# The output projection of the prompt as seven block products, with operand sums in DRAM

## The chip, the cores and the metric

The kernel runs on one core of a Trainium2 chip. The metric is the device time of one execution in microseconds (us). Single runs of the kernel before took 2335.16 to 2336.0 us, with a median of 2335.55 us over 3 runs.

## What is computed

One layer of a streaming encoder: RMS norm of x, one input projection into eight parts, stick-breaking attention (8 heads) beside retention (8 heads), a gated per-head norm of both, one output projection, and a norm with a residual. The part that the change touches is the end:

```python
def merge(o_sb, o_r, gate_sb, gate_r, g_sb, g_r, w_out):
    y_sb = head_rms_norm(o_sb, g_sb, gate_sb.dtype) * jax.nn.silu(gate_sb)
    y_r = head_rms_norm(o_r, g_r, gate_r.dtype) * jax.nn.silu(gate_r)
    y = jnp.concatenate([y_sb, y_r], axis=-1)
    return jnp.einsum('bte,ed->btd', y, w_out)
...
        xp = xp + rms_norm(out, norm_post[l])
```

It is done for 1024 prompt frames (8 tiles of 128 rows) and for 8 x 16 sample frames (one tile, "the sample"). y has 2048 columns: 16 blocks of 128, blocks 0 to 7 from the attention heads and 8 to 15 from the retention heads. w_out is 2048 x 2048.

## The kernel before

Every large product is made three times, since an f32 operand is split into a high part (rounded to the format fp32r) and the low rest: hi x hi, hi x lo, lo x hi. `split` (L139 to L141) does it for a weight block: ACT writes the high part (tile `wh`), DVE subtracts it (tile `wl`). The blocks come by SP's queue into `wr`. All three tags live in the pool `wp` with four buffers each (L118), so that the weights run at most four blocks ahead of TensorE at each of the two stages: landed, and converted.

The rows are done in two groups: group 1 has prompt tiles 0 to 3 and the sample, group 2 tiles 4 to 7. In a group each of the eight heads goes through its projections in an order written out by hand (`order`, L207): rq, rk, rv, rg, ret, q, k, v, sg, x. A projection (`products`, L297) uses one weight block of 256 KB for twelve products of 512 columns. The work of the branches, retention and attention, is cut into steps of generators (`Job`, L167) that `tick` (L172) takes up after so many products of TensorE: a `yield 28` means "go on after 28 ticks". `place` (L163) ties an instruction behind the last product in its engine's order. DRAM scratch tiles take the finished y: `s_y[group][block]`, and `s_ys` for the attention blocks of the sample. A scheduler decides the final order on each engine.

The output stage (from L1185 on) works on three chunks of three row tiles: (0, 1, 2), (4, 5, 6) and (3, sample, 7). `fetch` brings a chunk's y from DRAM and converts it, `out_panel` (L1205) makes one panel of 512 columns: for each of 16 blocks of w_out, three tiles x three products (L1222, L1223, L1224). A panel's results are squared by ACT (L1275) and multiplied with the gain by DVE (L1278), `close` scales the finished chunk and adds x (L1304) in steps placed between products of the next chunk. Of the last chunk the last 256 columns are done tile by tile (L1349 to L1351), with weights that `keep_last` has converted before, so that each tile's norm, scaling and stores can follow it.

In terms of block products: rows in two halves (tiles 0 to 3, tiles 4 to 7), y's columns in two halves, w_out's columns in halves too, so the prompt takes eight products of half matrices.

## Time and profile before

| what | value |
|---|---|
| median of 3 runs | 2335.55 us |
| lowest and highest | 2335.16 and 2336.0 us |
| span of the profiled execution | 2332.0 us |
| instructions in it | 39220 |
| first and last start of L1222 | 1922.8 and 2305.7 us |
| DMA, mean | 179 GB/s, 418.55 MB |

The profiled execution has no time of its own on the page, only its span, from its first to its last instruction; the median of the runs lies 3.55 us above it, which is what lies around the span. Engines are PE (TensorE's products), PEld (its weight loads, which run beside the products), DVE (VectorE), ACT (ScalarE), POOL (GpSimd) and SP (the DMA queue); "L302" is line 302 of the kernel. A group's row gives line, engine, operation, tile written and tiles read, shape, count, then busy us and mean ns of one, then the idle time before it and what ended it.

### The profile page before, as it was taken

Reading aid. Unit: us, or ns where it says so; the run is one execution under the profiler, and the core shown is the slowest. Engines: PE = TensorE matmul, PEld = TensorE weight load, DVE = VectorE, ACT = ScalarE, POOL = GpSimd, SP = SyncE. Lnnn points to the kernel's source line nnn. Section 1 sums busy time; section 2 is a strip of 40 time slices with the busy share of each in tenths; the row PEclk is TensorE's granted clock in tenths of the full one; section 3 lists DMA queues with packets and bytes.
Section 4 is the critical chain, followed back from the end, with each engine's and each line's share of the span. In section 5 each row is a group of like instructions: output and inputs, shape, how many; then the busy total and the mean of one; then the engine's idle time right before and its main releaser. Section 6 shows DMA issues by size and latency. Waiting matters only on the chain.

```text
span 2332.0 us, 39220 instructions
## 1 busy us (share of the span) xinstructions
PE 2304.9 (99%) x14256; PEld 2054.3 (88%) x14256; DVE 1336.2 (57%) x2642; ACT 892.7 (38%) x1880; POOL 513.4 (22%) x747
## 2 busy tenths in 40 slices
PE   7999999999999999999999999999999999999998
PEld 7999999999999999998888888888888888888888
DVE  8246564556555564556756655665665566555544
ACT  6323332333333242333443433434343344534342
POOL 2123241414223141423321311122032130010000
PEclk9999999999999999999999999999999999999999
DMA  7659686787869677798966656565565576757564
GB/s 251 166 132 232 165 187 171 187 199 169 204 154 206 175 180 186 172 225 215 225 174 159 154 152 154 136 158 150 150 159 149 138 186 199 239 177 225 173 213 134
DMA packets 696161, 418.55 MB, mean 179 GB/s; under 512 B 234880, under 2 KB 646784, under 8 KB 693536
## 3 DMA queue, kind: packets, MB, share of 16 engines
q1 hardware_dynamic: 632240, 316.27, 51.9%
q0 software_dynamic: 28528, 79.33, 13.9%
q10 hardware_dynamic: 35200, 20.45, 3.1%
q8 instruction: 111, 1.82, 0.3%
q14 instruction: 82, 0.67, 0.1%
HBM read 336.24 MB, written 79.69 MB: 178 GB/s over the span
## 4 chain that ended last, share of the span: by engine, by line
PE 94%; DVE 2%; issue 2%; ACT 1%; DMA 0%; POOL 0%; DVEq 0%; ACTq 0%; POOLq 0%
PE acc L302 51%; PE accn L361 12%; PE a L1222 5%; PE a L1223 5%; PE a L1224 5%; PE accx L389 4%; PE pa L693 3%; PE z L660 2%; PE pd L829 1%; PE zc L764 1%; PE rs L851 1%; DVE kp L603 1%; PE pS L884 1%; PE pa L869 1%; PE pa L874 1%
## 5 line engine op out<-in xcount | busy, mean ns | idle before, releaser
L141 DVE TENSOR_TENSOR wl<-wr,wh 128x512 fp32r<-128x512 f32 (+1 forms) x576 | 392.4, 684 | 561.8 <-ACT wh L140 545.8
L302 PE MATMUL acc<-mh,wl 128*128 128x256 f32 (+2 forms) x2304 | 662.5, 340 | 0.0
L302 PE MATMUL acc<-ml,wh 128*128 128x256 f32 (+2 forms) x2304 | 660.0, 339 | 0.8 <-DVE p0u L153 0.8
L302 PE MATMUL acc<-mh,wh 128*128 128x256 f32 (+2 forms) x2304 | 660.7, 339 | 0.0
L140 ACT ACTIVATE wh<-wr 128x512 fp32r<-128x512 f32 (+1 forms) x576 | 360.3, 626 | 771.8 <-PE acc L302 399.6
L302 PEld LDWEIGHTS acc<-ml,wh 128*128 128x128 f32 x2304 | 421.2, 188 | 36.3 <-issue 6.6
L302 PEld LDWEIGHTS acc<-mh,wl 128*128 128x128 f32 x2304 | 421.1, 188 | 36.4 <-issue 8.2
L302 PEld LDWEIGHTS acc<-mh,wh 128*128 128x128 f32 x2304 | 421.7, 188 | 34.5 <-issue 6.6
L745 POOL DMA_DIRECT2D kc<-cache_sb_k x256 | 166.5, 655 | 283.1 <-DVE kcT L776 131.7
L361 PE MATMUL accn<-whn,mh 128*128 128x256 f32 x768 | 223.9, 292 | 0.0
L1222 PE MATMUL a<-wh,mh 128*128 128x512 f32 (+1 forms) x576 | 219.7, 381 | 0.1
L1223 PE MATMUL a<-wl,mh 128*128 128x512 f32 (+1 forms) x576 | 219.2, 380 | 0.0
L1224 PE MATMUL a<-wh,ml 128*128 128x512 f32 (+1 forms) x576 | 219.1, 380 | 0.0
L361 PE MATMUL accn<-wln,mh 128*128 128x256 f32 x768 | 217.0, 283 | 0.0
L361 PE MATMUL accn<-whn,ml 128*128 128x256 f32 x768 | 216.9, 283 | 0.0
L361 PEld LDWEIGHTS accn<-whn,mh 128*128 128x128 f32 x768 | 146.6, 191 | 9.8 <-issue 7.9
L361 PEld LDWEIGHTS accn<-wln,mh 128*128 128x128 f32 x768 | 146.6, 191 | 0.3
L603 DVE TENSOR_TENSOR_SCAN kp<-kp 128x640 f32<-128x640 f32 (+6 forms) x72 | 108.4, 1505 | 66.5 <-POOL kp L592 63.9
L361 PEld LDWEIGHTS accn<-whn,ml 128*128 128x128 f32 x768 | 146.4, 191 | 0.0
L1222 PEld LDWEIGHTS a<-wh,mh 128*128 128x128 f32 x576 | 108.3, 188 | 20.8 <-DVE sg L406 0.3
L1224 PEld LDWEIGHTS a<-wh,ml 128*128 128x128 f32 x576 | 108.3, 188 | 20.5
L1223 PEld LDWEIGHTS a<-wl,mh 128*128 128x128 f32 x576 | 108.3, 188 | 20.3
(209 smaller groups left out, 2968.5 us busy)
## 6 DMA issues: line engine op xcount, KB each, us to landing
wr<-w_in SPq DMA_DIRECT2D x384, 256.0 KB, 3.9
wr<-w_out SPq DMA_DIRECT2D x184, 256.0 KB, 3.6
vc<-cache_sb_v SPq DMA_DIRECT2D x64, 512.0 KB, 7.5
wrn<-w_in SPq DMA_DIRECT2D x80, 256.0 KB, 3.7
kc<-cache_sb_k SPq DMA_DIRECT2D x256, 64.0 KB, 3.9
kc<-cache_sb_k POOLq DMA_DIRECT2D x256, 64.0 KB, 4.2
wrx<-w_in SPq DMA_DIRECT2D x48, 256.0 KB, 3.0
xt<-x_prompt SPq DMA_DIRECT2D x8, 1024.0 KB, 5.4
```

The source lines that it names most:

```text
L140: nc.scalar.activation(hi, src, AF.Copy)
L141: nc.vector.tensor_tensor(lo, src, hi.bitcast(F32), ALU.subtract)
L302: last = nc.tensor.matmul(a[:, :m], lhs[:, j, :], rhs[w][:, j, o : o + m], start=(w == 0 and j == 0 and n == 0), stop=(w == KT // WQ - 1 a ...
L361: product[0] = nc.tensor.matmul(a, lhs[q][:, jj, ts], rhs[:, j, :], start=(w == 0 and j == 0 and n == 0 and t % 2 == 0), stop=(w == KT // ...
L389: product[0] = nc.tensor.matmul(banks[t], lhs[q][:, j, ts], rhs, start=(k == 0 and n == 0), stop=(k == KT - 1 and n == 2))
L603: nc.vector.tensor_tensor_scan(rev, rev, rev, 1.0, ALU.mult, ALU.bypass)
L660: mm = nc.tensor.matmul(z[:, :c], q2[a][:, i * P : (i + 1) * P], k2[b][:, :c], start=(m == 0), stop=(m == 2))
L693: nc.tensor.matmul(po[:, :P], at[:, j, :], rest["vn"][:, j, :], start=(j == 0), stop=(j == t))
L745: (nc.gpsimd if i < 2 else nc.sync).dma_start(kc[32 * i : 32 * i + 32, :].rearrange("p (k d) -> p k d", d=32), cache_k[0, 2 * c + j, s * 5 ...
L1222: nc.tensor.matmul(a[:, :width], hi[q][:, j, ts], wh, start=(k == 0), stop=False)
L1223: nc.tensor.matmul(a[:, :width], hi[q][:, j, ts], wl, start=False, stop=False)
L1224: product[0] = nc.tensor.matmul(a[:, :width], lo[q][:, j, ts], wh, start=False, stop=(k == KT - 1))
```

## The change

The prompt's output projection is done with seven instead of eight half-matrix products, in Winograd's form of Strassen's scheme. The products are named 1 to 7. Product 1 takes y's block a11 (tiles 0 to 3, attention columns) and the w_out block of the same rows, 2 takes a12, 4 takes a22; 3, 5, 6 and 7 take sums of blocks of y (s4, S1, S2, s3). The matching sums of w_out's blocks (names "5", "6", "7", "4") are made in group 2 by `column_sums`: loads of w_out, four DVE operations on 128 x 512 for each of 16 steps, and a store of 1 MB to the scratch `s_t`. The sums of y are made by `row_sums` wholly in DRAM, by copies and adding DMAs of 1 MB on POOL's queue: for the first half of the heads in group 2, for the second half in the output stage.

The output stage runs four units (half of the heads, half of w_out's columns); a unit has seven products, each with four weight blocks x four row tiles x three products of 512 columns. Products 1, 6, 7, 4 add up in one set of PSUM banks, 5 and 3 in another. `give` adds a bank into the f32 tiles `o` of the output in SBUF, and squares and multiplies by the gain at the last of the addends. The y operands stay in four slots and two extra tiles; `fill` loads the next one into a slot when the product that used it is done, and `cut` converts it two products later. The last unit has the order 1, 2, 6, 5, 3, 7, 4, its product 4 runs tile by tile (`outer`), and the rows of x are loaded into the slots that have become free.

The sample's part leaves the output stage. Its 16 blocks are loaded beside group 2's operands (`sample_rows`), and four new steps o4 to o7 (`do_o`), each 512 columns x 16 weight blocks x three products, stand in group 2's written order; the raw result goes to DRAM and is finished in the output stage (`finish_sample`).

```diff
-                "rq3 rk3 ret3 rg3 q3 k3 sg3 rq4 rk4 ret4 rg4 q4 k4 x4 sg4 rq5 rk5 ret5 q5 k5 rg5 sg5 "
-                "rq6 rk6 ret6 q6 k6 x6 sg6 rq7 q7 k7 rg6 rk7 ret7 rg7 sg7"
+                "rq3 rk3 ret3 rg3 q3 k3 sg3 rq4 rk4 ret4 rg4 q4 k4 x4 sg4 o4 rq5 rk5 ret5 q5 k5 rg5 sg5 o5 "
+                "rq6 rk6 ret6 q6 k6 x6 sg6 rq7 q7 k7 rg6 rk7 ret7 o6 o7 rg7 sg7"
...
+            def do_o(self):
...
+                for k in range(KT):
+                    wr = take_w()
...
+                    split(wh, wl, wr)
+                    q, j = divmod(k, WQ)
+                    for n, (a, b) in enumerate(((hi, wh), (hi, wl), (lo, wh))):
+                        product[0] = nc.tensor.matmul(
+                            bank, a[q][:, j, NB_TOK:], b, start=(k == 0 and n == 0), stop=(k == KT - 1 and n == 2)
+                        )
+                        tick()
...
+        def column_sums():
+            for u in range(2):
+                for k in range(H):
+                    r = run["tq"].tile([P, 2, 2, 512], F32, name="tr", tag="tr")
+                    t = run["tq"].tile([P, 4, 512], F32, name="ts", tag="ts")
...
+                    yield D_LATE
+                    place(nc.vector.tensor_tensor(t[:, 0], r[:, 0, 0], r[:, 0, 1], ALU.subtract))
+                    nc.vector.scalar_tensor_tensor(t[:, 1], t[:, 0], -1.0, r[:, 1, 1], ALU.mult, ALU.subtract)
+                    yield D_FIN
...
+                    place(nc.gpsimd.dma_start(s_t[u][:, k], t))
+                    yield D_LATE
...
+        def row_sums(q):
...
+            for name, first, more in (("S1", a21, a22), ("s3", a11, a21), ("S2", s["S1"], a11), ("s4", s["S2"], a12)):
+                place(nc.gpsimd.dma_start(s[name], first))
+                yield D_TI[1]
+                place(nc.gpsimd.dma_start(s[name], more, accum_op=ALU.add))
+                yield D_TI[1]
...
+        USES = {"1": "a11", "2": "a12", "6": "S2", "5": "S1", "7": "s3", "3": "s4", "4": "a22"}
...
+            def one(k, p):
+                wh, wl = blocks[k]
+                ts = slice(p * P, (p + 1) * P)
+                for n, (a, b) in enumerate(((hi, wh), (hi, wl), (lo, wh))):
+                    product[0] = nc.tensor.matmul(
+                        banks[p], a[:, k, ts], b,
...
+                if done and k == H // 2 - 1:
+                    done(p)
...
+            if outer:
+                for p in range(4):
+                    for k in range(H // 2):
+                        one(k, p)
...
+        def finish_first():
+            tot = rp.tile([P, 4], F32, name="tot")
+            nc.vector.tensor_reduce(tot, ssq[:, 0:4], mybir.AxisListType.X, ALU.add)
+            rs = inv_rms(rp, tot, D, "out")
+            for t in range(4):
+                for c in range(4):
+                    scale(t, c, rs[:, t : t + 1], nc.gpsimd)
...
+                if final and name == "3":
+                    finish_first()
+                if final and name == "7":
+                    rest[0] = rest_of(x2)
...
+                if name == "2":
+                    fill("s4", mix["a12"], half, nc.gpsimd)
+                    due.setdefault(step + 2, []).append("s4")
...
+                elif (half, u) == (0, 1):
+                    if name == "1":
+                        drain(job)
+                    fill(used, mix[used], 1, nc.gpsimd)
+                    due.setdefault(step + 2, []).append(used)
```

How the instructions stand on the engines, at three places.

DVE, near the end of group 2. Before, in the projections of the last head: `kp` and `be` belong to the attention's scan, `sc`, `ro` and `S` to the retention, `rg` is a gate, `ml` the operand's low part, `wl` the low part of a weight block:

```order
L853 TENSOR_TENSOR sc<-rs,dT 128x128
L406 TENSOR_TENSOR rg<-rg,acc_20507 128x512
L853 TENSOR_TENSOR sc<-rs,dT 128x128
L889 SCALAR_TENSOR_TENSOR S<-S,pS 128x128
L204 TENSOR_TENSOR ml_20651<-ml_20651,mh_20650 128x2x384
L878 SCALAR_TENSOR_TENSOR ro<-pa,dec,ro 128x128
L204 TENSOR_TENSOR ml_20651<-ml_20651,mh_20650 128x2x384
L853 TENSOR_TENSOR sc<-rs,dT 128x128
L878 SCALAR_TENSOR_TENSOR ro<-pa,dec,ro 128x128
L575 STREAM_TRANSPOSE kp<-be 128x6x4x32
L889 SCALAR_TENSOR_TENSOR S<-S,pS 128x128
L141 TENSOR_TENSOR wl_20827<-wr_20818,wh_20826 128x512
```

and now, in o6 (`wlo` is the low part of a weight block of do_o):

```order
L615 SCALAR_TENSOR_TENSOR kp<-kp 128x896
L138 TENSOR_TENSOR wlo<-wr_21066,who 128x512
L616 TENSOR_TENSOR be<-be,kp 128x896
L138 TENSOR_TENSOR wlo<-wr_21075,who 128x512
L138 TENSOR_TENSOR wlo<-wr_21084,who 128x512
L138 TENSOR_TENSOR wlo<-wr_21093,who 128x512
L138 TENSOR_TENSOR wlo<-wr_21102,who 128x512
L138 TENSOR_TENSOR wlo<-wr_21112,who 128x512
L138 TENSOR_TENSOR wlo<-wr_21121,who 128x512
L587 STREAM_TRANSPOSE kp<-be 128x5x4x32
```

Weight blocks' splits now stand close behind each other here, with the attention's operations between them.

DVE, where the finished rows of the output are scaled (`out` or `o_...` with `xr`, the rows of x). Before, in the middle of the next chunk:

```order
L1304 SCALAR_TENSOR_TENSOR out<-out,out3r,xr 128x512
L141 TENSOR_TENSOR wl_22170<-wr_22167,wh_22169 128x512
L1304 SCALAR_TENSOR_TENSOR out<-out,out3r,xr 128x512
L141 TENSOR_TENSOR wl_22187<-wr_22184,wh_22186 128x512
L141 TENSOR_TENSOR wl_22202<-wr_22199,wh_22201 128x512
L1304 SCALAR_TENSOR_TENSOR out<-out,out3r,xr 128x512
L141 TENSOR_TENSOR wl_22219<-wr_22216,wh_22218 128x512
```

and now, near the end of the program, the last of finish_first's sixteen (L1362), then the takes of product 7 (L1351) and its gains (L1357), then the splits of product 4:

```order
L1362 SCALAR_TENSOR_TENSOR o_2_21770<-o_2_21770,outr,xr 128x512
L1362 SCALAR_TENSOR_TENSOR o_3_21771<-o_3_21771,outr,xr 128x512
L1351 SCALAR_TENSOR_TENSOR o_3_21775<-a_23508,o_3_21775 128x512
L1351 SCALAR_TENSOR_TENSOR o_3_21779<-a_23509,o_3_21779 128x512
L1351 SCALAR_TENSOR_TENSOR o_3_21783<-a_23510,o_3_21783 128x512
L1357 TENSOR_TENSOR o_3_21775<-o_3_21775,gpost 128x512
L1357 TENSOR_TENSOR o_3_21779<-o_3_21779,gpost 128x512
L1357 TENSOR_TENSOR o_3_21783<-o_3_21783,gpost 128x512
L1351 SCALAR_TENSOR_TENSOR o_3_21787<-a_23511,o_3_21787 128x512
L138 TENSOR_TENSOR wl_24095<-wrt,wh_24094 128x512
L138 TENSOR_TENSOR wl_24101<-wrt,wh_24100 128x512
```

Before, the scales stood singly between splits; now sixteen stand in a row, ahead of three of the last product's four splits.

POOL, at the start of the output stage. Before, the last y is stored, the gain loaded, then the outputs are stored:

```order
L562 DMA s_o_7_4_20909<-ro 128x16x32
L640 DMA s_y_15_142<-rg 128x512
L562 DMA s_o_7_4_21103<-so 128x16x32
L640 DMA s_y_7_134<-sg 128x512
L1244 DMA gpost<-norm_post 128x2048
```

and now, from the gain on (`s_S_1_112`, `s_S_1_113`, `s_s_1_114` and `s_s_1_115` are S1, S2, s3 and s4 of the second half, `s_y_104` and `s_y_105` y of groups 1 and 2, L1241 a copy, L1243 an adding DMA, `ml_21550` the slot of a12):

```order
L1336 DMA gpost<-norm_post 128x2048
L1241 DMA s_S_1_112<-s_y_105 128x2048
L1241 DMA s_s_1_114<-s_y_104 512x1x512
L1243 DMA s_S_1_112<-s_y_105 128x2048
L1243 DMA s_s_1_114<-s_y_105 128x2048
L1241 DMA s_S_1_113<-s_S_1_112 16x16384
L1405 DMA out<-rawc 128x512
L1401 DMA xrc<-x_sample 128x512
L1243 DMA s_S_1_113<-s_y_104 512x1x512
L1400 DMA rawc<-s_raw 128x512
L1241 DMA s_s_1_115<-s_S_1_113 16x16384
```

Between the gain and the next operand loads stand eight DMAs of the row sums, in which one reads what an earlier one wrote, and the sample's small ones.

More of the change, by code (lines that the diff above doesn't have):

```diff
@@ L1233, in tile_hybrid_step, with four @@
+        def four(pool):
+            return [pool.tile([P, 512], F32, name="a3", tag=f"acc{n % 2}") for n in range(4)]
+        chain = four(accp)
+        mixed_product("1", chain, 1, REFILL[3])
         for kind in ("ret", "sb"):
@@ L1372, in tile_hybrid_step, with give @@
-        out_project(chunk3[0] + chunk3[1], kept=keep)
+        outs = [[rp.tile([P, 512], F32, name=f"o{t}_{c}") for c in range(4)] for t in range(PT)]
+        ssq = rp.tile([P, PT, 4], F32, name="ssq3")
+        job = Job(row_sums(1), 2)
+        given = {}
+        xrs = {}
+        def give(t, c, bank):
+            o = outs[t][c]
+            n = given[t, c] = given.get((t, c), 0) + 1
+            end = n == (2 if t >= 4 and c % 2 == 0 else 4)
+            if n == 1:
+                nc.scalar.activation(o, bank, AF.Copy)
+            elif end and t >= 4:
+                nc.vector.scalar_tensor_tensor(o, bank, -1.0, o, ALU.mult, ALU.subtract)
+            else:
+                nc.vector.tensor_tensor(o, bank, o, ALU.add)
+            if end:
+                sq = rp.tile([P, 512], F32, name="sq3", tag="sq3")
+                nc.scalar.activation(sq, o, AF.Square, accum_out=ssq[:, t, c : c + 1])
+                nc.vector.tensor_tensor(o, o, gpost[:, c * 512 : (c + 1) * 512], ALU.mult)
@@ new lines, in last_scale @@
+        def last_scale(t, c):
+            v, r, u = (rp.tile([P, 1], F32, name=f"last{x}", tag=f"last{x}", bufs=2) for x in "vru")
+            nc.vector.scalar_tensor_tensor(
+                v, ssq[:, t, c : c + 1], -4.0 / D, rest[0][:, t - 4 : t - 3], ALU.mult, ALU.add
+            )
+            nc.scalar.activation(r, v, AF.Sqrt, scale=-1.0)
+            nc.vector.reciprocal(r, r)
+            nc.vector.scalar_tensor_tensor(u, r, r, v, ALU.mult, ALU.mult)
+            nc.vector.scalar_tensor_tensor(u, u, 3.0, r, ALU.add, ALU.mult)
+            return u
```

351 lines of the change are left out of this document (177 added, 174 removed).

## The prediction

> **What bounds the kernel now.** I read the page first, then the time windows of the output stage, then single rows. The page's head, its shares and the chain that ended last:
>
> ```profile
> span 2332.0 us, 39220 instructions
> PE 2304.9 (99%) x14256; PEld 2054.3 (88%) x14256; DVE 1336.2 (57%) x2642; ACT 892.7 (38%) x1880; POOL 513.4 (22%) x747
> PEclk9999999999999999999999999999999999999999
> PE 94%; DVE 2%; issue 2%; ACT 1%; DMA 0%; POOL 0%; DVEq 0%; ACTq 0%; POOLq 0%
> ```
>
> TensorE is the chain, at full granted clock. "Busy" is not "at its peak", so the second view is windows (us from:to, length, busy us and count of PE, PEld, DVE, ACT, POOL, granted clock, DMA share, GB/s): most of group 2, two stretches of the output stage, and the end.
>
> ```profile
> 1300.00:1900.00 600.00, 598.88 (x2888) 502.69 (x2887) 363.50 (x638) 240.09 (x499) 125.39 (x144) 1.00 0.58 151
> 2000.00:2100.00 100.00, 100.00 (x443) 82.78 (x442) 54.29 (x92) 41.65 (x81) 6.39 (x12) 1.00 0.62 204
> 2100.00:2200.00 100.00, 100.00 (x443) 82.81 (x442) 48.76 (x83) 43.34 (x84) 0.58 (x2) 1.00 0.62 195
> 2300.00:2332.00 32.00, 23.51 (x196) 23.30 (x195) 15.32 (x37) 5.97 (x20) 0.00 (x0) 0.94 0.37 121
> ```
>
> TensorE has no gaps; VectorE (DVE) is busy 0.61 of group 2 and about half of the output stage. So every product that is dropped is worth its pace, as long as the engines that feed TensorE keep up with a denser schedule. The pace is the distance between starts, not the duration, in the timeline of the output stage; the 256-wide pace is in the chain; the counts are in the groups by shape:
>
> ```profile
> 2100.44 0.39 PE L1222 MATMUL a<-wh,mh 128*128 128x512 f32 x1
> ...
> 2101.12 0.39 PE L1222 MATMUL a<-wh,mh 128*128 128x512 f32 x1
> 2317.87 0.12 PE a L1350
> 2317.99 0.12 PE a L1351
> L1222 PE MATMUL a<-wh,mh 128*128 128x512 f32 x528 | 206.1, 390 | 0.1
> L1222 PE MATMUL a<-wh,mh 128*128 128x256 f32 x48 | 13.6, 283 | 0.0
> L1349 PE MATMUL a<-mh 128*128 128x256 f32 x48 | 13.6, 283 | 0.0
> ```
>
> Three 512-wide products start in 0.68 us (L1222 to the next L1222), so 0.227 us each; a 256-wide one takes 0.12 us.
>
> **Part 1: products removed.** L1222, L1223 and L1224 have 528 wide and 48 narrow products each, L1349 to L1351 48 narrow each: 1584 wide and 288 narrow, 359.0 + 34.6 = 393.6 us. After: 4 units x 7 names x 4 blocks x 4 tiles x 3 = 1344, and 4 x 16 x 3 = 192 for the sample, all wide: 1536 x 0.2267 = 348.2 us. **Gain 45.4 us**, all on the path. The Trainium skill, "TensorE: Matmul & The Clock Gate", section "Back-to-back issue gap", gives about N/2.4 + 2.5 ns when warm, 215.8 ns at 512; by it this gain would be some 4 us smaller. The measured pace is 0.227 us, 5% above the page, and I go by the row.
>
> **Part 2: the sample's part, do_o.** A weight block (256 KB: load, wh on ACT, wl on DVE) feeds nine products in the old panels, 2.04 us of TensorE, and twelve in a projection, 2.72 us. In do_o it feeds three, 0.68 us. What a block costs the others (landing of the loads, then the two conversions):
>
> ```profile
> wr<-w_out SPq DMA_DIRECT2D x184, 256.0 KB, 3.6
> DMA to landing us min/median/max: 2.3/3.6/7.7
> L140 ACT ACTIVATE wh<-wr 128x512 fp32r<-128x512 f32 x560 | 353.7, 632 | 761.6 <-PE acc L302 399.6 <-PE a L1224 150.7 <-issue 80.6
> L141 DVE TENSOR_TENSOR wl<-wr,wh 128x512 fp32r<-128x512 f32 x560 | 385.7, 691 | 552.6 <-ACT wh L140 536.6 <-PE acc L302 7.7 <-DMA ml<-s_y 4.0
> ```
>
> The pool wp has four buffers of each. A buffer of wr comes round in 3.6 + 0.63 + 0.69 + about 0.2 for the signals = 5.1 us; in that time four blocks arrive, and TensorE uses four in 2.7 us. So each round of four is 2.4 us short. Four blocks converted and four landed stand ready when do_o begins, so two rounds are free. o4 and o5 (16 blocks each): two short rounds, 4.8, and 1.8 until the first block of the next step comes, 6.6 each. o6 and o7 stand back to back: six short rounds, 14.4 + 1.8 = 16.2. **Cost 29 us.** Lower bound by DVE alone: its other work in group 2 is 0.61 less the splits (0.69 per 2.72 us), 0.36 per us; with 11.0 us of splits in 10.9 us of TensorE it is short by some 4 us per step, and at the smallest landing time, 2.3, the round is 1.1 us short ten times: 11 to 16. Upper bound: loads that queue behind each other, 5.5 us (inside the row's 7.7): 4.3 x 10 = 43. I take the median's value. The 64 loads now stand on SP's queue among the turn-in reads of group 2 (in o7, ahead of the last head's ro<-s_rk); who waits for those is the retention of the same head, due 30 ticks (7 us) later, so I add nothing for it.
>
> **Part 3: the end.** What follows the last product now (the chain; then DVE's timeline and a group):
>
> ```profile
> 2323.39 0.13 PE a L1351
> 2326.60 1.33 DVE out L1304 x2
> 2324.74 0.22 DVE L1298 SCALAR_TENSOR_TENSOR lastu<-lastr,lastv 128x1 f32<-128x1 f32 x1
> 2325.19 2.74 DVE L1304 SCALAR_TENSOR_TENSOR out<-out,lastu,xr 128x512 f32<-128x512 f32 x4
> L1278 DVE TENSOR_TENSOR out<-a,gpost 128x512 f32<-128x512 f32 x33 | 22.5, 690 | 1.3 <-ACT sq L1275 0.5
> ```
>
> 8.6 us pass from the last product (2323.4) to the end (2332.0), 4.1 of them after DVE's last. After the change all 32 blocks of 512 are scaled within the last two products. By the order of instructions, the 16 scales of finish_first stand on DVE ahead of the takes of product 7 and ahead of three of the four wl splits of the last product, 4; and that product runs tile by tile, so its first tile needs all four splits. Let T0 be the end of product 3 on TensorE, which alone would need 2 x 10.9 for 7 and 4: end T0 + 21.8 + 8.6 = 30.4. DVE from T0: 32 scales at (2.74 - 0.75)/3 = 0.66 (the lone scale is 0.75 in the chain), 21; 21 takes and gains at 0.65, 13.6; five splits, 3.4; about 25 small ones at 0.18, 4.5; together 42.7. It waits about 5 us more (ACT's roots; the first two tiles of product 4, whose last split is ready only near T0 + 25, so TensorE idles some 12 us). 42.7 + 5 + 4.1 = T0 + 52: **cost 21 us**; 16 if those waits vanish, 26 if the granted clock, 0.94 in the last window, halves over product 4 (10.9 / 2).
>
> **Part 4: the row sums in DRAM.** Nothing like a DRAM-to-DRAM copy or an adding DMA is in the trace. The nearest rows, 1 MB each:
>
> ```profile
> xt<-x_prompt SPq DMA_DIRECT2D x8, 1024.0 KB, 5.4
> xr<-x_prompt SPq DMA_DIRECT2D x8, 1024.0 KB, 6.9
> ```
>
> On POOL's queue in the output stage stand, after product 2 of unit 1 (T = 22 us from its first product): the loads of s4, s3, a22 and gpost, then row_sums(1), where S1 copy, S1 add, S2 copy, S2 add, s4 copy each wait for the one before, and only then the load of a12, which unit 2 needs. At 0.62 share for 204 GB/s the queues' full rate is 329 GB/s; weights take 96, which leaves 4.5 us per MB. S1's copy lands near 22 + 1 + 5 x 4.5 + 2.4 = 48; four dependent steps at 6.9 and s3's add between them, 32, give 80; a12 lands behind s4's add at 92 and is converted by 95. ACT and DVE wait for it with two blocks split, which TensorE has used at 7 x 10.9 + 5.4 = 82: 13 us. At 5.4 us a step the load is in time, cost 0; with adds that take twice a copy, 30. **I take 10.** row_sums(0) runs in group 2 with 34 ticks (7.7 us) per step, about one landing: the affine selects behind it on POOL, for which DVE's scans wait, are then held up little.
>
> **Part 5: the rest.** Column sums add 64 DVE operations of about 0.69 (44 us) and 48 large DMAs, spread over group 2, where DVE has 0.39 of 600 us free; TensorE's four blocks of lead cover a DVE delay of up to 10 us. Cost 4, bounds 0 and 15 (each of 16 loads waited for by DVE for 1 us). The old fetches, kept panel and their DMAs lie beside TensorE now: their removal gains nothing.
>
> **Sum.** -45.4 + 29 + 21 + 10 + 4 = +18.6 on the span: 2350.6. The median shown, 2335.55, lies 3.55 above the span. Forecast **2354 us**. A measurement of this kernel can tell about 0.2%, 4.7 us, from no change.
>
> **Rivals.**
> - *Faster: the feed keeps up.* Loads land in 2.3 us during do_o because the other queues are quiet there (the window shows 151 GB/s in group 2, far from 329), and the adds are as fast as the 5.4 row. Then -45.4 + 12 + 16 + 0 + 0 = -17: 2318. It decides where the four terms together fall under 45 (under 41, measurably). For it: TensorE never waited in the windows shown. Against: DVE's own count in parts 2 and 3. Chance 0.17.
> - *No change*: the terms come to 41 to 50, near 2335. Chance 0.11.
> - *Half clock.* The last window shows 0.94 where TensorE is idle for 8.5 of 32 us, so idle stretches lower the granted clock. do_o would leave TensorE half idle. At half clock a product takes 0.45 us, a do_o step 21.8: 10.9 lost in each of four, and some 1.7 in the step after three of them, 49 instead of 29: 2374. The Trainium skill states this rule in the same page, "Part 1: The HAM clock gate": an idle window of about 3.4 us halves the clock until a busy one has passed; it speaks against this change. By it the 12 us gap at the end would count, while the gaps of some 2.4 us in do_o are shorter than a window. Or the adds take twice a copy: +20, the same time. Chance 0.20.
> - The forecast itself, 2336 + 5 up to about 2370: 0.52.
>
> That the change does not do what it says is ruled out by the order: the products are 1536.
>
> **Range and chances.** 2322 leaves out about half of the faster case, 2390 a small part of the slow one. Faster by over 0.2% has 0.17, within it 0.11, slower 0.72.
>
> **What would show it.** Products at 0.227 us in the panels: part 1. In do_o, ACT waiting on the weight loads and TensorE on ACT or DVE, some 6 us per step and more in o6 and o7: part 2. A gap before the last product with 16 scales on DVE, and about 18 us from the last product to the end: part 3. A TensorE gap at unit 2's first product with ACT waiting on a12: part 4. I am wrong if do_o shows steps near 11 us, or if the last product follows product 7 without a gap.

## The result

| kernel | median, us | lowest to highest | runs |
|---|---|---|---|
| before | 2335.78 | 2335.16 to 2336.91 | 4 |
| changed | 2402.09 | 2397.93 to 2403.82 | 4 |

The change makes the kernel slower: ratio 1.0279, 95% interval 1.0264 to 1.0293. The forecast was 2354 us with a range of 2322 to 2390, so the sign was right and the time lies outside of the range. The page's head and the chain of the changed kernel:

```profile
span 2400.9 us, 38629 instructions
PE 2294.6 (96%) x13920; PEld 2021.6 (84%) x13920; DVE 1423.1 (59%) x2772; ACT 914.1 (38%) x1889; POOL 544.0 (23%) x809
PEclk9999999999999999999999999999999999989998
PE 77%; issue 7%; DMA 7%; DVE 5%; ACT 1%; POOL 1%; SPq 0%; DVEq 0%; ACTq 0%; POOLq 0%
```

TensorE has 336 products fewer and is busy 10 us less (2294.6 against 2304.9), in a span that is 68.9 us longer. It is 77% of the chain instead of 94%; DMA and DVE are on it now, and the granted clock is down to eight tenths in two of the last five slices.

**Where the time went.** The products of group 2's projections are the same in both kernels, so I count them back from the last one and compare the starts of the same product in the two timelines. The last one, by the rows of the projection's line in the kernel before and in the changed one:

```profile
L302 PE MATMUL acc<-mh,wl x2304: 274/338/499, 22.4 to 1922.5; 128*128 128x256 f32 x127, 128*128 128x512 f32 x64, 128*128 128x384 f32 x1
```

```profile
L314 PE MATMUL acc<-mh,wl x2304: 274/338/774, 23.3 to 2035.3; 128*128 128x256 f32 x127, 128*128 128x512 f32 x64, 128*128 128x384 f32 x1
```

Group 2 ends 112.8 us later, of which 43.5 are the sample's 192 products. The lag at other products (us; the later kernels are told below, and in s5 and s13 the o steps stand elsewhere, so that for them the rows only name the place):

| place (start before) | changed | s5 | s7 | s10 | s13 |
|---|---|---|---|---|---|
| start of group 2 (1109.6) | 2.0 | 2.9 | 1.8 | 5.0 | 3.1 |
| before o4 (1639.3) | 22.7 | 40.4 | 3.3 | 23.4 | 7.5 |
| behind o4 (1703.9) | 40.5 | 52.7 | 19.9 | 35.8 | 19.4 |
| behind o5 (1753.7) | 64.1 | 62.7 | 44.3 | 51.5 | 29.7 |
| before o6 (1893.9) | 63.4 | 73.6 | 43.6 | 50.8 | 53.0 |
| behind o7 (1906.1) | 115.3 | 73.6 | 95.1 | 89.2 | 57.1 |
| end (1922.5) | 112.8 | 77.6 | 92.8 | 86.7 | 60.5 |

"Behind" a step is the next place at which I read the lag, not the next product: directly behind o4 the lag is 42.2 us, of which 1.7 are made good up to the place at 1703.9.

In the output stage the first product starts at 1922.8 before and at 2035.5 now, the last ends at 2323.5 and 2383.8, the span ends at 2332.0 and 2400.9. Between first and last product 7.1 us were not the 393.6 of products before, and 43.6 are not the 304.7 now. So:

| part | forecast | measured |
|---|---|---|
| products removed | -45.4 | -45.4 |
| o4 to o7 beyond their products (17.8 + 23.6 + 51.9 - 43.5) | +29 | +49.8 |
| group 2 outside of them (22.7 - 2.0) | +4 | +20.7 |
| two gaps in the output stage, with the slow clock and small waits around them | +10 | +27.5 |
| gap before the last product 9.0, and 17.1 instead of 8.5 us behind it | +21 | +17.6 |
| rest (group 1 +2.0; -0.7 and -2.5 between the o steps and behind them) | 0 | -1.2 |
| sum | +18.6 | +69.0 |

**o5, as an example of do_o.** TensorE and, behind it, ACT in the timeline of the changed kernel (start, duration, idle time before it and what ended that):

```profile
1762.40 0.34 PE L672 MATMUL z<-kh,ql 128*128 128x384 f32 x1
1765.81 0.50 PE L1179 MATMUL acco<-who,mh 128*128 128x512 f32 x1 [3.06 <-ACT who L137]
...
1771.12 0.79 PE L1179 MATMUL acco<-wlo,mh 128*128 128x512 f32 x1 [1.63 <-DVE wlo L138]
...
1774.17 0.63 PE L1179 MATMUL acco<-wlo,mh 128*128 128x512 f32 x1
1774.59 0.63 PE L1179 MATMUL acco<-who,ml 128*128 128x512 f32 x1
```

```profile
1759.41 0.63 ACT L137 ACTIVATE who<-wr 128x512 fp32r<-128x512 f32 x1 [0.67 <-DVE oT L587]
1765.12 1.27 ACT L137 ACTIVATE who<-wr 128x512 fp32r<-128x512 f32 x2 [5.08 <-DMA wr<-w_out]
...
1774.18 0.63 ACT L137 ACTIVATE who<-wr 128x512 fp32r<-128x512 f32 x1 [2.44 <-DMA wr<-w_out]
```

The blocks come late (5.1 us of waiting for the load), TensorE idles 3.1 us, and then its products start every 0.42 us (1774.17 to 1774.59) instead of 0.23, though none of them waits. That lasts from 1767.8 to 1777.6: the granted clock halves after the gap, as a window of that stretch shows (PEclk, DMA share and GB/s last):

```profile
1767.50:1777.50 10.00, 8.03 (x17) 5.46 (x18) 7.44 (x11) 4.42 (x9) 3.57 (x4) 0.50 0.64 204
```

Summed over the 512-wide products that wait for nothing and start over 0.33 us apart at this halved clock, it costs some 7 us in the stretches of o4 to o7, and some 15 in the whole changed kernel; in the kernel before there is no such product. The Trainium skill, "TensorE: Matmul & The Clock Gate", section "Part 1: The HAM clock gate", states half speed after an idle window of about 3.4 us and full speed after a busy one. The trace agrees on the halving; but 1.8 us of idle time inside o6, between other short gaps, were enough, and the slow stretch in o5 lasts nearly 10 us, with a gap of 1.6 us in it.

**The two gaps in the output stage.** POOL's queue, then DVE, then TensorE, in the timeline around the end of unit 1. `s_S` and `s_s` are the row sums, `rawc` the sample's raw rows, `ml<-s_y` the load of a12:

```profile
2067.36 0.55 POOL L1241 DMA_DIRECT2D s_S<-s_y  x1
...
2086.34 0.88 POOL L1243 DMA_DIRECT2D s_S<-s_y  x1 [17.68 <-DMA s_S<-s_y]
...
2098.26 0.53 POOL L1241 DMA_DIRECT2D s_S<-s_S  x1 [7.95 <-DMA s_S<-s_y]
...
2107.64 1.22 POOL L1243 DMA_DIRECT2D s_S<-s_y  x1 [7.69 <-DMA s_S<-s_S]
2108.31 1.12 POOL L1400 DMA_DIRECT2D rawc<-s_raw  x1
2118.71 0.52 POOL L1241 DMA_DIRECT2D s_s<-s_S  x1 [9.29 <-DMA s_S<-s_y]
...
2127.96 1.38 POOL L1251 DMA_DIRECT2D ml<-s_y  x1
```

```profile
2108.59 0.69 DVE L138 TENSOR_TENSOR wl<-wrt,wh 128x512 fp32r<-128x512 f32 x1 [3.29 <-ACT wh L137]
2119.11 0.69 DVE L1403 TENSOR_TENSOR rawc<-rawc,gpost 128x512 f32<-128x512 f32 x1 [9.83 <-DMA rawc<-s_raw]
...
2120.50 1.29 DVE L138 TENSOR_TENSOR wl<-wrt,wh 128x512 fp32r<-128x512 f32 x2
```

```profile
2121.24 0.79 PE L1270 MATMUL a<-wl,a22h 128*128 128x512 f32 x1 [8.85 <-DVE wl L138]
...
2145.65 0.80 PE L1270 MATMUL a<-wh,mh 128*128 128x512 f32 x1 [7.75 <-ACT wh L137]
```

Gap 1: the load of the sample's raw rows is issued at 2108.3, right behind an add of the row sums (1 MB) that had waited 7.7 us for its copy. The add has landed when POOL goes on at 2118.7, and the load of 256 KB behind it when DVE goes on at 2119.1. So DVE stands 9.8 us on that load, with the split of a weight block next in its order, and TensorE waits 8.9 us for that split. The scheduler had put the sample's finishing there, well ahead of the place in the code. Gap 2 is the forecast one: a12 is loaded last, at 2127.96, lands at 2141, and ACT's splits for unit 2 stand behind its conversion.

### The profile page after: what moved, and what is told of

The parts are those of the page before. It is cut to its first block, busy times and chain, and to the rows that moved or that the text cites. A ratio compares the mean times of both kernels' runs of the same rounds, so it can differ in the third digit from the quotient of the medians.

```text
span 2400.9 us, 38629 instructions
## 1 busy us (share of the span) xinstructions
PE 2294.6 (96%) x13920; PEld 2021.6 (84%) x13920; DVE 1423.1 (59%) x2772; ACT 914.1 (38%) x1889; POOL 544.0 (23%) x809
## 4 chain that ended last, share of the span: by engine, by line
PE 77%; issue 7%; DMA 7%; DVE 5%; ACT 1%; POOL 1%; SPq 0%; DVEq 0%; ACTq 0%; POOLq 0%
PE acc L314 46%; PE accn L373 11%; PE a L1270 8%; PE accx L401 3%; PE pa L705 2%; PE z L672 2%; DMA wr<-w_out 1%; PE pd L841 1%; PE zc L776 1%; DMA s_s<-s_y 1%; DVE o L1362 1%; DVE kp L615 1%; DMA be<-s_bd 1%; DVE kp L587 1%; DMA out<-rawc 1%
## 5 line engine op out<-in xcount | busy, mean ns | idle before, releaser
L138 DVE TENSOR_TENSOR wl<-wr,wh 128x512 fp32r<-128x512 f32 x432 | 296.2, 690 | 430.8 <-ACT wh L137 426.3
L137 ACT ACTIVATE wh<-wr 128x512 fp32r<-128x512 f32 x432 | 271.5, 632 | 631.5 <-PE acc L314 368.0
L1270 PE MATMUL a<-wh,mh 128*128 128x512 f32 x320 | 126.2, 394 | 10.9 <-ACT wh L137 8.2
L615 DVE TENSOR_TENSOR_SCAN kp<-kp 128x640 f32<-128x640 f32 (+6 forms) x72 | 108.1, 1502 | 41.0 <-POOL kp L604 38.4
L1270 PE MATMUL a<-wl,mh 128*128 128x512 f32 x320 | 126.1, 394 | 2.3 <-DVE wl L138 2.3
L1270 PE MATMUL a<-wh,ml 128*128 128x512 f32 x320 | 125.7, 393 | 0.0
L587 DVE STREAM_TRANSPOSE kp<-be 128x640 f32<-128x640 f32 (+6 forms) x72 | 95.3, 1323 | 7.8 <-DMA be<-s_bd 5.6
L705 PEld LDWEIGHTS pa<-vn,kp 128*128 128x128 f32 x576 | 78.9, 196 | 21.8 <-DVE kp L587 16.6
L138 DVE TENSOR_TENSOR wln<-wrn,whn 128x512 fp32r<-128x512 f32 x80 | 54.9, 688 | 68.2 <-ACT whn L137 65.2
```

The lines of the kernel that those rows point to most:

```text
L137: nc.scalar.activation(hi, src, AF.Copy)
L138: nc.vector.tensor_tensor(lo, src, hi.bitcast(F32), ALU.subtract)
L587: place(nc.vector.transpose(dst.rearrange("p (k b j) -> p k j b", j=4, b=32), raw))
L615: nc.vector.tensor_tensor_scan(rev, rev, rev, 1.0, ALU.mult, ALU.bypass)
L705: nc.tensor.matmul(po[:, :P], at[:, j, :], rest["vn"][:, j, :], start=(j == 0), stop=(j == t))
L1270: product[0] = nc.tensor.matmul(banks[p], a[:, k, ts], b, start=(name in "125" and k == 0 and n == 0), stop=(k == H // 2 - 1 and n == 2), ...
```

## The experiments

Differences are against the changed kernel's median, 2402.09.

**s1, s2, s3: what stands on POOL's queue.**

```diff
-                if n == 1:
+                if n == 2:
                     next(sample, None)
...
-                nc.gpsimd.dma_start(raw, s_raw[:, c, :])
+                place(nc.gpsimd.dma_start(raw, s_raw[:, c, :]))
...
-                    fill("a12", mix["s4"], half if u == 0 else 1, nc.gpsimd)
+                    fill("a12", mix["s4"], half if u == 0 else 1, nc.sync)
```

The first two hunks (with `place` around the xrc load and the first DVE operation too) are s1, the last is s2, all of them s3.

> The finishing of the sample (loads rawc and xrc on POOL's queue, two DVE operations, a store, four times) is moved to the third unit, and its operations are tied behind products so that the scheduler can't pull them ahead. Theory A (DVE stands in its order on a rawc load that is itself stuck on POOL's queue behind the dependent DMAs of the row sums; TensorE waits for the split behind it): the gap of 11.9 us in the last product of unit 1 (2109.4 to 2121.2) is gone and DVE waits no more for rawc. Since the a12 load stays last on POOL's queue and lands at about 2141, the gap before unit 2's product 2 grows by as much, so the time falls little: 2392 to 2402 us. Theory B (the gap comes from weight blocks that land late because the DMA engines are full): the gap stays, the time is within 4 us of 2402.

> Only the load of a12 into its slot moves from POOL's queue to SP's. Theory A (a12 waits in POOL's order for the row sums, not for DMA bandwidth): it lands before unit 2 needs it, the gap of 7.8 us before unit 2's product 2 goes, with the slow clock behind it some 9 to 11 us: 2391 to 2394. Theory B (the DMA engines are full, so it lands as late from another queue, or the weights behind it on SP's queue come late instead): within 4 us of 2402.

> Both of the edits before: the sample finished in unit 3, and a12 loaded by SP's queue. Theory A (two separate stalls that both come from the order on POOL's queue): the two gaps go, with the slow clock behind them 20 to 25 us: 2377 to 2382. Theory B (full DMA engines): less than 8 us.

Measured: s1 2392.20 us (-9.9), s2 2393.81 (-8.3), both as theory A had it; s3 2384.80 (-17.3), less than theory A's 20 to 25, and its runs go from 2373.86 to 2387.55. TensorE's waits from 2040 to 2150, in s1:

```profile
PE a L1270 <- ACT wh L137: 11.9, 2, 10.0
```

and in s3:

```profile
PE a L1270 <- ACT o L1349: 1.6, 1, 1.6
PE a L1270 <- ACT wh L137: 1.3, 1, 1.3
PE a L1270 <- DVE wl L138: 0.8, 2, 0.6
```

With gap 1 gone the wait for a12 grows from 7.8 to 10.0; with both edits no wait of the output stage before the end is over 1.6 us. So the mechanism of theory A holds: two stalls that both come from the order on POOL's queue. In the profiled executions first to last product of the output stage takes 323.4 us in s3 and 348.3 in the changed kernel; the profiled execution of s3 is the fastest of its four by 10.7 us, so these 25 us are more than the medians give.

**s4, s8: the end.** In s4 ACT multiplies the 16 blocks by the norm and POOL adds x; in s8 the sixteen stay on DVE behind the last splits.

```diff
-            nc.vector.scalar_tensor_tensor(o, o, rs, xrs[t][:, cs], ALU.mult, ALU.add)
+            if t < 4:
+                nc.scalar.activation(o, o, AF.Copy, scale=rs)
+                nc.gpsimd.tensor_tensor(o, o, xrs[t][:, cs], ALU.add)
...
             if outer:
+                finish_first()
                 for p in range(4):
...
-                if final and name == "3":
-                    finish_first()
```

(The first hunk is s4; the others, with the scales of tiles 0 to 3 tied behind a product, are s8.)

> The scales of tiles 0 to 3 (16 blocks, finish_first) are made by ACT (times the norm) and POOL (plus x) instead of by DVE. Theory A (these sixteen stand in DVE's order ahead of the takes of product 7 and of the splits of the last product): the gap before the last product (8.9 us lost with the clock) goes, and the end after the last product is shorter, 13 us instead of 17.5: 11 to 14 us gained, 2388 to 2391. Theory B (the late rows of x, which POOL's queue loads into the freed slots, are what is waited for): within 4 us of 2402.

> The sixteen scales of tiles 0 to 3 stand on DVE behind the takes of product 7 and all four splits of the last product, instead of ahead of them. Theory A (DVE's work from product 3 to the end, 43 us, sets the end, in whatever order): the gap before the last product goes (8.9 us), but the stretch from the last product to the end grows by about as much, since DVE is also idle while product 7 runs: 2398 to 2408. Theory B (the order alone costs it): the gap goes and the end stays near 17.5 us behind the last product, 2392 to 2394.

Measured: s4 2412.93 us (+10.8), s8 2402.18 (+0.1). In s4 neither theory held. ACT's sixteen take 9.9 us in a row, and DVE waits 5.1 us for a square that stands behind them. Then DVE itself is slow; DVE and POOL in its timeline:

```profile
2377.42 3.62 DVE L138 TENSOR_TENSOR wl<-wrt,wh 128x512 fp32r<-128x512 f32 x1
2380.97 3.63 DVE L1357 TENSOR_TENSOR o<-o,gpost 128x512 f32<-128x512 f32 x1
2384.52 3.62 DVE L138 TENSOR_TENSOR wl<-wrt,wh 128x512 fp32r<-128x512 f32 x1
```

```profile
2377.99 2.49 POOL L1364 TENSOR_TENSOR o<-o,xr 128x512 f32<-128x512 f32 x2
2381.53 2.51 POOL L1364 TENSOR_TENSOR o<-o,xr 128x512 f32<-128x512 f32 x2
```

A split that takes 0.69 us takes 3.62 beside POOL's additions; four takes of product 7 (L1351), which read one operand from PSUM, need 2.7 us in all beside them. In s8 TensorE's gap of 6.7 us before the last product is gone and the end is not earlier: from the last product to the end it takes 25.2 us (2376.0 to 2401.2) instead of 17.1. That is theory A: DVE's amount of work sets the end, in whatever order.

**s5, s10: what do_o waits for.** s5 spreads the 64 blocks, s10 leaves out three of four loads (the sample's output is another then).

```diff
+            if now[0] in HOSTS:
+                next(run["o"])
...
+            if gi == 1 and (step, h) in HOSTS:
+                for load in loads[0]:
+                    to_load += [load, o_loads.pop(0)]
...
-                    wr = take_w()
+                    if k % 4 == 0:
+                        wr = take_w()
```

(The last hunk alone, with a quarter of the loads in the list, is s10. HOSTS are 16 projections from rq4 to k7.)

> The same 64 weight blocks and 192 products of the sample, but no block stands beside another of its kind: one follows each of the four weight blocks of 16 projections of heads 4 to 7 (fifteen products for two blocks, 3.4 us, instead of three for one, 0.68 us). In the trace of the changed kernel the four steps o4 to o7 lose some 50 us beyond their own 43.5 us of products. Theory A (three products don't cover the landing and the two conversions of their block): nearly all of it is regained, 40 to 48 us, 2354 to 2362. Theory B (in group 2 the engines DVE and ACT and the queues have no room for 64 more blocks wherever they stand): at most half, 2377 or more.

> The four steps o4 to o7 as in the changed kernel, but only every fourth weight block is loaded; the 64 conversions and 192 products stay (three of four use the wrong block, so the sample's output is another). It tells landing from conversion. In the trace of the changed kernel the steps lose some 50 us. Theory A (the round of four buffers, landing plus conversions, is what is short): without most of the landings 30 to 45 us are regained, 2357 to 2372. Theory B (DVE and ACT have no room for a conversion every 0.68 us beside their other work): at most 15, 2387 or more.

Measured: s5 2378.87 us (-23.2), s10 2374.37 (-27.7). By the table of lags the o steps of s10 cost 12.4 + 15.7 + 38.4 - 43.5 = 23 us beyond their products instead of 49.8: the landing of three loads in four is some 27 us of it, with some 6 us of the halved clock among them. The 23 us that are left are the conversions beside DVE's and ACT's other work, with the loads that stay. Each theory holds for about half, and neither number is met. In s5 group 2 ends 35 us earlier than in the changed kernel, though the whole gains only 23, between its two theories: o6 and o7 had covered the last head's branches. Now more of these fall into the output stage, and its first three products lose 23.3 us beyond their pace instead of 5.2.

**s6, s7, s11, s12: the column sums.** Of `column_sums` only the distances change: ticks from load to first use, and from store to next load.

```diff
                         ))
-                    yield D_LATE
+                    yield 60
                     place(nc.vector.tensor_tensor(t[:, 0], r[:, 0, 0], r[:, 0, 1], ALU.subtract))
...
                     place(nc.gpsimd.dma_start(s_t[u][:, k], t))
-                    yield D_LATE
+                    yield 60
```

(The first hunk is s6, the second s12. In s7 the job isn't started and products 4 to 7 load plain blocks of w_out, so their results are others. In s11 the two are 46 and 10, with the edits of s9 below and later places for the sample's blocks: from sg4 on, two each beside rg6 and rk7.)

> In the column sums the first DVE operation is placed 60 ticks (13.6 us) behind its load instead of 28 (6.3 us); the loads land in 7.4 us at the median. In group 2 outside of o4 to o7 the changed kernel loses some 22 us. Theory A (DVE stands in its order on loads that have not landed): 10 to 16 us are regained, 2386 to 2392. Theory B (the 64 operations, or the 32 MB of loads and stores beside the turn-in reads, are the cost, wherever DVE waits): within 5 us of 2402.

> The column sums are left out (loads, DVE operations, stores); products 4 to 7 use plain blocks of w_out, loaded as often and in the same size, in place of the sums. This bounds what the column sums cost in all. Theory A (nearly all of the 22 us that group 2 loses outside of o4 to o7 come from them, and part of the loss inside, since DVE is less busy): 20 to 35 us regained, 2367 to 2382. Theory B (that loss comes from the sample's rows and the row sums of the first half, which stay): under 10 us, above 2392.

> The four edits of the run before, rearranged: the sample's blocks go beside later projections (from sg4 on, two each in the last two hosts, rg6 and rk7, where the last head's branches leave TensorE waiting), and the column sums' round is 64 ticks as in the changed kernel, with 46 of them between load and use, so that they end before the sample's blocks begin. Theory A (the 10 us lost from 1520 to 1572 came from column sums and sample blocks at the same time): 8 to 14 us better than 2353, 2339 to 2345. Theory B (DVE is full wherever the blocks stand): within 4 us of 2353.

> In the changed kernel's column sums only the distance from the store of 1 MB to the next load of 1 MB is changed, from 28 to 60 ticks; the first DVE operation stays 28 ticks behind its load. It tells two causes apart that s6 changed at once (60 ticks between load and use also make the round longer, 96 ticks instead of 64). Theory A (DVE stands on loads that have not landed): the waits stay, no more than 5 us regained, 2397 to 2405. Theory B (a store of 1 MB, the next load of 1 MB and the turn-in of the scan fill the DMA engines together, and the weight blocks behind them land late): 12 to 20 us regained, as in s6, 2382 to 2390.

| run | ticks load to use, store to load | us | lag before o4 or the first host, less group 1's |
|---|---|---|---|
| changed | 28, 28 | 2402.09 | 20.7 |
| s7 | no sums | 2382.88 | 1.5 |
| s6 | 60, 28 | 2383.03 | 1.8 |
| s12 | 28, 60 | 2388.12 | 7.3 |
| s11 | 46, 10 | 2362.45 (beside s9's edits) | 28.2 |

The sums cost 19 us (s7, just under its theory A), and s6 regains all of that without leaving anything out, more than its theory A. In the changed kernel TensorE's waits up to o4 are on operands that DVE makes for the branches, above all 8.6 us on transposes of `kp` and 4.1 on the copy of `rv`; none is on a weight block. ACT waits for some that land late (5.4 us at 1232.8). Ahead of two of the three longest, DVE stands on a load of the sums that has not landed (`tr`):

```profile
1433.21 0.69 DVE L1227 TENSOR_TENSOR ts<-tr 128x512 f32<-128x512 f32 x1 [3.09 <-DMA tr<-w_out]
1434.30 0.80 PE L314 MATMUL acc<-mh,wh 128*128 128x512 f32 x1 [4.12 <-DVE rv L1156]
...
1477.08 0.69 DVE L1227 TENSOR_TENSOR ts<-tr 128x512 f32<-128x512 f32 x1 [4.06 <-DMA tr<-w_out]
1482.52 1.16 PE L705 MATMUL pa<-vn,kp 128*128 128x128 f32 x8 [3.00 <-DVE kp L587]
```

That is theory A's wait, but it is not the only one: in s11 DVE waits for no load of the sums (no such row among its waits), and the loss is the largest; s11 met neither of its theories. ACT, SP's and POOL's queues in s11, and its windows (PEclk, DMA share and GB/s last):

```profile
1259.76 0.63 ACT L137 ACTIVATE wh<-wr 128x512 fp32r<-128x512 f32 x1 [8.06 <-DMA wr<-w_in]
```

```profile
1245.93 0.81 SPq L1236 DMA_DIRECT2D tr<-w_out  x2
1246.79 0.43 SPq L586 DMA_DIRECT2D s_be<-be  x1
1247.91 13.60 SPq L231 DMA_DIRECT2D wr<-w_in  x5
```

```profile
1246.20 0.57 POOL L1246 DMA_DIRECT2D s_t<-ts  x1 [5.36 <-DVE ts L1244]
1246.77 0.98 POOL L593 DMA_DIRECT2D be<-s_be  x1
```

```profile
1250.00:1255.00 5.00, 5.00 (x23) 4.12 (x22) 1.78 (x5) 0.40 (x2) 0.00 (x0) 1.00 1.00 375
1255.00:1260.00 5.00, 4.51 (x20) 3.39 (x19) 0.00 (x0) 0.24 (x1) 0.00 (x0) 1.00 1.19 216
```

A store of 1 MB, the next load of 1 MB, the scan's turn-out and turn-in are issued within 1 us; the DMA engines are full for 10 us, and a weight block issued behind them keeps ACT waiting 8.1 us. DVE's splits, the scan's transposes and TensorE follow. In the changed kernel, over most of the stretch of the sums, the share rises from 0.61 to 0.88, and TensorE loses 10 us; before and changed kernel:

```profile
1228.00:1461.00 233.00, 232.46 (x1134) 195.61 (x1133) 143.97 (x252) 90.85 (x191) 45.90 (x51) 1.00 0.61 153
```

```profile
1228.00:1461.00 233.00, 222.29 (x1053) 185.22 (x1052) 163.98 (x286) 85.81 (x182) 47.12 (x62) 0.98 0.88 262
```

s12 moves only the next load away from the store, and 14 us come back, within theory B's 12 to 20. But it does not tell the two causes apart, since DVE's waits for `tr` go too (0.8 us instead of 11.0). And s6 speaks against store and load alone: there the next load is issued as close behind the store as in the changed kernel (4.9 and 5.5 us at the median), and yet the loss is gone. What s6 and s12 share is a round of 96 ticks instead of 64: fewer bytes per time (in the window above the share is 0.83 in both), and loads that have landed when DVE comes to them. Which of the two gave the time back is not shown, nor what makes s6 5 us the better.

**s9, s13, s16: the edits together.** s9 is spread + 60 ticks + both edits of s3. s13 takes s11's places for the blocks, with 60 and 28 ticks. s16 (with the end of s15 below) has the doubled sixteen beside rk4, rg4, q4 and k4 instead.

```diff
+    HOSTS = {x: 1 for x in (
+        ("sg", 4), ("rq", 5), ("rk", 5), ("q", 5), ("k", 5), ("rg", 5), ("sg", 5), ("rq", 6),
+        ("sg", 6), ("rq", 7), ("q", 7), ("k", 7),
+    )}
+    HOSTS.update({("rg", 6): 2, ("rk", 7): 2})
```

> The four edits that each regained time stand together: the sample's blocks spread over 16 projections (23 us alone), the column sums' operations 60 ticks behind their loads (19 alone), the sample finished in unit 3 and a12 loaded by SP's queue (17 together). Theory A (separate stalls, which add): 2402 - 59 = 2343, 2336 to 2350, and the end of the last product stays as it was, with DVE's work behind it. Theory B (the stalls share their cause, so that a later one takes up what an earlier one gives back): 2355 or more.

> The four edits with the sample's blocks beside the later projections (as in s11) and the column sums with 60 ticks between load and use and 28 behind the store (as in s9). Theory A (s11 lost by the column sums' round of 64 ticks alone, while the later places are better by some 9 us than those of s9): 2340 to 2346. Theory B (the later places collide with the sums, which end later again): 2351 or more.

> As s15, but the sixteen blocks that stood doubled beside the last two hosts go beside rk4, rg4, q4 and k4 instead, one each. In s13 the last 50 us of group 2 lose 10 us. Theory A (two blocks to a host are too dense): 4 to 8 us better than s15. Theory B (at that place they covered the last head's branches, and the earlier places run into the column sums, which end near 1611): 3 to 10 us worse than s15.

Measured: s9 2353.10 us, ratio to before 1.0074 (1.0060 to 1.0088); s13 2333.35, ratio 0.9994 (0.9985 to 1.0003); s16 2344.47, ratio 1.0035 (1.0021 to 1.0049). s9 missed its 2343 and lies near B: in its first hosts, from rq4 on, the sums still run (they end near 1618), and 8 to 11 us are lost there, against 4 to 5 in s5, whose sums have ended by then. As in s5, the first three products of the output stage lose 22.8 us. s13 is better than its theory: 17.0 us of group 2's lag are not the sample's products, instead of 69.3. s16 is 16.7 us worse than s15, more than its theory B said: in the profiled executions 7 us go in group 2 and 14 in the output stage, where more of the last head's branches then fall.

**s14, s15: DVE's work at the end, taken to the DMA engines.** On top of s13. In s14 the rows of x are copied to the output beforehand, ACT multiplies the 16 blocks by the norm, and adding DMAs bring them there. s15 does so for tiles 0 and 1 alone (the hunk is of s15).

```diff
+                        if p < 2:
+                            place(nc.scalar.activation(o, o, AF.Copy, scale=rs[:, p : p + 1]))
+                            nc.gpsimd.dma_start(y_rows(p)[:, c * 512 : (c + 1) * 512], o, accum_op=ALU.add)
+                        else:
+                            scale(p, c, rs[:, p : p + 1], nc.gpsimd)
```

> On top of s13: DVE no longer scales tiles 0 to 3. The rows of x are copied to the output in unit 4's predecessor, ACT multiplies the 16 blocks by the norm between the tiles of the last product, behind all four splits, and adding DMAs on POOL's queue add them to the output. Theory A (as s8 suggested, DVE's work from the end of product 3 sets the end; 16 x 0.66 = 10.6 us of it go): the gap of 6.7 us before the last product goes and the end comes 8 to 12 us earlier, 2322 to 2326. Theory B (ACT's sixteen, or the adding DMAs' landing, take DVE's place at the end): 2330 or more.

> As s14, but only tiles 0 and 1 (8 blocks) go by ACT and adding DMAs; DVE scales tiles 2 and 3. In s14 DVE was done at 2318.2, 7 us earlier than in s13, but the 16 adding DMAs kept the DMA engines full to the end at 2335.4. Theory A (the end is the later of DVE's work and the adding DMAs): with 8 blocks each DVE ends 3 to 4 us earlier than in s13 and the adds some 10 us earlier than in s14, so 3 to 5 us better than s13: 2328 to 2331. Theory B (every adding DMA slows the other stores as well): 2333 or more.

Measured: s14 2337.66 us, ratio 1.0017 (1.0007 to 1.0028), by its theory B; s15 2327.77, ratio 0.9964 (0.9952 to 0.9977), by its theory A. In s14 the gap before the last product is gone and DVE is done at 2318.2, but the end is at 2335.4. Its DMA issues of the last 50 us, and two windows behind DVE's last instruction:

```profile
out<-o POOLq DMA_DIRECT2D x16, 256.0 KB, 11.3
out<-o SPq DMA_DIRECT2D x16, 256.0 KB, 11.9
```

```profile
2320.00:2325.00 5.00, 0.00 (x0) 0.00 (x0) 0.00 (x0) 0.00 (x0) 0.00 (x0) 0.50 1.11 254
2325.00:2330.00 5.00, 0.00 (x0) 0.00 (x0) 0.00 (x0) 0.00 (x0) 0.00 (x0) 0.50 1.09 299
```

and the same issues in s13, where POOL's are plain stores:

```profile
out<-o POOLq DMA_DIRECT2D x16, 256.0 KB, 4.0
out<-o SPq DMA_DIRECT2D x16, 256.0 KB, 2.7
```

With adding DMAs the stores of the other tiles take 11.9 us instead of 2.7, and nothing but DMA runs for 15 us. Half of them balances the two (8.0 and 6.8 us): s15, the only kernel here that is faster than the kernel before, by 0.36%.

## Why the forecast was wrong

- **Part 1** is right: 1536 products, and where nothing waits they start every 0.227 us.
- **Part 2 failed in size**, 29 forecast, 49.8 measured, above its upper bound of 43. The step that failed is the round of four buffers: "A buffer of wr comes round in 3.6 + 0.63 + 0.69 + about 0.2". o4 came out near the forecast (6.9 against 6.6; 8.6 directly behind it); o5 cost 12.7 and o6 with o7 30.1 instead of 6.6 and 16.2. The loads landed in 3.4 to 4.4 us at the median of a step, not far from the 3.6, but several in o5 and o7 took 6 to 7. And DVE's `wlo` started 0.8 us after the end of ACT's `who` on average and up to 4.0, where the sum had about 0.2 for all signals. s10 splits the 49.8: 27 go with three loads in four, 23 stay without them. And the clock: I had written that "the gaps of some 2.4 us in do_o are shorter than a window"; some 7 us of halved clock are in these steps.
- **Part 5 failed**: "TensorE's four blocks of lead cover a DVE delay of up to 10 us", 4 forecast, 20.7 measured, above the bound of 15. That lead is one of weight blocks, and TensorE waited for none of them: it stood on operands of the branches that DVE had not made, 4.1 us right behind a DVE wait of 3.1. The cost was not DVE's operations (s6 keeps them all, at 1.8 us) but the sums' DMAs in too short a round. Their loads landed in 7.4 us at the median, with 28 ticks, 6.3 us, before the use, so that DVE waited 11.0 us for them; and in s11 a burst of them held up the weight blocks. How the 19 us divide between the two stays open.
- **Part 4**: the a12 gap came where and why it was forecast, at 12 us with its slow clock, against 10. That it came so near is in part luck: a12 landed 105.6 us behind the first product instead of 92, and TensorE was 20.5 us late itself by then. What failed is the list of what queues behind the waiting DMAs: I saw "the sample's small ones" among them in the order and priced only the load of a12. DVE waits for one of those small loads, and weight splits stand behind DVE: another 11 us (s1 to s3). The two gaps and what lies around them, 27.5, stay under the upper bound of 30, but that was set for one wait.
- **Part 3** is right: 17.6 against 21, from DVE's work; product 3 ends near 2352.9 and the span 48.0 us later, against 52. s8 and s15 bear out that it is the work and not the order.
- **The rivals.** "Half clock" had the nearest time, 2374, and by the sign its mechanism took place, but with some 15 us in all it is not what lifts the time to 2402. What does is four stalls: the o steps, the column sums, the order on POOL's queue and DVE's work at the end. With edits to the first three, s13 gives 69 us back. Two of the terms lay above their own upper bounds (49.8 against 43, 20.7 against 15), and the top of the range, 2390, lay below the sum of the upper bounds, some 2404.

## What to carry to other kernels

Fewer products pay only where their operands come as cheaply as before: here 8 us of the saving of 45 came out (s15), and only once the blocks with little work stood among blocks with much, the column sums had a longer round, nothing that DVE waits for stood behind a chain of dependent DMAs on a queue, and a part of the scales at the end was taken off DVE. Before costing a moved step, list for each in-order queue what stands behind each of its waits, small loads included, and look at where the scheduler put them, not where the code has them. A mean DMA share says little of a burst; read windows of 5 us. And a lead in weight blocks covers no wait for other operands: go through what TensorE waits for in each stage.

## What the hardware showed beyond that

- A DVE operation with two operands in SBUF takes 3.62 us instead of 0.69 beside POOL's additions on the same kind of operands (s4), while ACT beside them keeps its 0.6. The Trainium skill, "SBUF — State Buffer", section "Who interferes with whom", says that such a DVE instruction contends with a POOL instruction that reads SBUF; the trace agrees, and the loser here was DVE, five times as slow.
- Adding DMAs of 256 KB land in 11.3 us where plain ones do in 4.0, and slow plain stores beside them from 2.7 to 11.9 us (s14, s13). In the changed kernel the row sums' adds of 1 MB took 9.1 to 14.2 us, median 10.5, and their copies inside DRAM 5.6 to 21.1, median 8.2, against 5.4 to 6.9 for the loads that I had taken as the nearest rows.
- The granted clock fell after gaps shorter than I expected: in o6 the products behind 1.8 us of idle time among other short gaps started 0.43 us apart.
